# Products of 512 columns issued as two of 256, and tiles that begin at multiples of 128 bytes

## The chip, the cores and the metric

The kernel runs on one core of one Trainium2 chip. The metric is the device time of one execution in microseconds (us), taken as the median of several runs. A profiled execution lies beside them; its rows are what the prediction is worked out from.

## The reference, cut to what matters

Four transformer blocks over 512 tokens of width 1024, in float32, one after the other: block 1 has latent and windowed attention, block 2 forgetting and chunked attention, blocks 3 and 4 a mixer of convolution, sparse attention, spatial gating and pooling. After each mixer comes an output projection, then a gated feed-forward layer of width 2816, then a norm. Nearly all of the arithmetic is products of a 512 x 1024 (or 512 x 2816) activation with a weight matrix.

```
x = layer_norm(ALPHA * x + mixer(x) @ w_out)               # blocks 1, 2
x = layer_norm(ALPHA * x + (silu(x @ w_gate) * (x @ w_up)) @ w_down)
...
x = x + rms_norm(mixer(rms_norm(x)) @ w_out)               # blocks 3, 4
gu = causal_dwconv(rms_norm(x) @ w_up)
x = x + rms_norm((gelu(gu[:half]) * gu[half:]) @ w_down)
```

## The kernel before, in words

**Split operands.** A float32 matrix is carried as two tiles in the type float32r, a high part and the rest (`split`, L229). A product of two such matrices is three products on TensorE: high with high, high with low, low with high, added up in one PSUM bank of 512 float32 columns. Weights arrive by DMA in `wraw`; ScalarE casts them to `whi` (L235) and VectorE subtracts to get `wlo` (L236), for 1024 columns at a time. Activations in this form are `xh` and `xl`, 128 partitions by 8 by 512.

**Every product goes through `mm` (L270, the instruction at L271).** `mm(out, a, b)` keeps the operand `a` in the array (the kept operand; the profile shows its load as LDWEIGHTS on PEld) and moves the columns of `b` through it (the moving operand). In the rows a product is written out<-moving,kept. The kept operand is at most 128 columns wide. Those who call it:

- `fm` (L273): weights are kept, `xh` and `xl` move, all 512 tokens at once (or, from `early`, 256 of them). For each of the 8 pieces of the inner dimension it issues (wh, xh), (wh, xl), (wl, xh). The feed-forward layer of blocks 3 and 4 (`ffn`, L1298) calls it for 22 pairs of weight blocks, the mixers through `fm_tile` (L285).
- `early` (L290): the first four weight blocks of a stage are multiplied with tokens 0 to 255 first, while the last tokens are still being normalised and transposed, and then with tokens 256 to 511.
- `tok_mm` (L303): activations are kept, 128 tokens at a time, and weights move. `out_proj` (L327) uses it with both halves of 512 columns for the output projections (8 steps) and the down projections (22 steps); the kept activations are split into `pr`, `pt`, and, near the end, `piece` tiles. `tok_proj` (L312) uses it for projections by token, with columns cut at 384, 260, 320 and 332 or 512.
- `product` (L522) in `quartered` (L503): the feed-forward layer of blocks 1 and 2 as seven products per unit with 256 moving columns; three of the seven move `pr` and `pt` or `piece` tiles (operands 4, 5, 6 of `room_for`, L490), the others parts of `xh` and `xl`.

Transposes (L430, L450, L699, L886 and others) are issued beside `mm`, with 128 moving columns. The attention products are float32 or have 64 rows.

**Order.** Each engine runs its instructions in the order in which the program issues them; `behind` (L373) places the transposes of the last tokens after a given product. The weights' DMAs go through the queue of SyncE. Nothing of this order is planned by costs.

**Where tiles lie.** Three pools: constants, all SBUF tiles (`tl`, L200, and `small`, L416), and PSUM banks. A pool hands out its space by tag, in the order of first use, each tile rounded up to 32 bytes. The constants end 64 bytes past a multiple of 128. So `xh`, `xl`, `room_a` and `piece` begin 64 bytes past one; `st` (64 bytes) puts `wraw`, `whi` and `wlo` on a multiple of 128; small tiles between them put `m`, `q`, `kf`, `x`, `pr` and `pt` 32 bytes past one. Slices of 128, 256 or 512 columns are multiples of 512 bytes and change nothing in that.

Of the kernel before, what the change touches and what calls it, by code (L numbers as in the profile page):

```python
# [9 lines left out]
F32 = mybir.dt.float32  # L10
F32R = mybir.dt.float32r
# [5 lines left out]
P = 128  # L17
# [10 lines left out]


TAIL, HELD, HEAD = 4, 2, 3  # L30
LAG = 1
EARLY = (1, 2)
CONV = 4
# [155 lines left out]
class Kernel:  # L189
    def __init__(self, ctx, tc, t, out, layers=4):  # L190
        self.nc, self.tc, self.t, self.out, self.layers = tc.nc, tc, t, out, layers
        pool = lambda n, b=1, **k: ctx.enter_context(tc.tile_pool(name=n, bufs=b, **k))
        self.const = pool("const")
        self.sb = pool("sb")
        self.ps = pool("ps", space=PSUM)
        self.n = 0
        self.setup()


    def tl(self, tag, shape, dt=F32, bufs=1):  # L200
        self.n += 1
        return self.sb.tile(shape, dt, tag=tag, name=f"{tag}_{self.n}", bufs=bufs)

    def arena(self):

# [9 lines left out]
    def setup(self):  # L215
        nc, t = self.nc, self.t
        self.c = {}
        for n in ("ident", "swap", "cmp_mask", "cmp_any", "pool_cnt"):
            self.c[n] = self.const.tile(list(t[n].shape), F32, name="c_" + n)
        self.ident = self.c["ident"]  # L220
        self.mhalf = self.const.tile([P, 8], F32, name="mhalf")
        nc.vector.memset(self.mhalf, -0.5)

    def load_const(self, *names):
        for n in names:
# [42 lines left out]
        return view(hi), view(lo)  # L268

    def mm(self, out, a, b, start=True, stop=True, **k):  # L270
        self.last_mm = self.nc.tensor.matmul(out, a, b, start=start, stop=stop, **k)  # L271

    def fm(self, out, w, x, cols=None):  # L273
# [53 lines left out]
    def out_proj(self, act, nk, src, use, order, first=None):  # L327
# [36 lines left out]
        for t in range(NT):  # L364
# [3 lines left out]
            later.append(use(t, ps[t]))  # L368
            if t >= LAG and later[0]:
                self.behind(later.pop(0))  # L370
# [45 lines left out]
    def small(self, name, bufs=1):  # L416
        src = self.t[name]
        self.n += 1
        x = self.sb.tile(list(src.shape), F32, tag="s_" + name[:-1], name=f"s_{name}_{self.n}", bufs=bufs)
        self.nc.sync.dma_start(x, src)  # L420
        return x

# [1061 lines left out]
```

## Time and profile before

| | |
|---|---|
| median of 3 runs | 2369.16 us (2368.55 to 2370.86) |
| the profiled execution, its own time | 2370.62 us |
| its span, first to last instruction | 2368.9 us |
| mean granted clock of TensorE | 0.995 of full speed |
| instructions | 33153, of them 13098 products and 13098 loads |
| DMA | 227.37 MB, mean 96 GB/s |

Reading: PE is TensorE's products, PEld its loads of the kept operand, DVE is VectorE, ACT ScalarE. Ends of products are modelled, and one product's time overlaps the next one's; the distance of two starts is what the array really needs from one to the next. Where a row of the timeline stands for several instructions (x2, x8), it gives the first start and the time to the last end.

### The profile page before, as it was taken

The numbers are of one execution on the slowest core, as the hardware profiler recorded it, in microseconds if no ns is written. First come the engines' busy times: TensorE is split into PE (matmuls) and PEld (weight loads), VectorE is DVE, ScalarE is ACT, GpSimd is POOL, SyncE is SP. The second block draws the span as 40 slices with busy tenths as digits, with TensorE's granted clock in tenths as the row PEclk, the third lists the DMA queues.
The fourth block names the chain that finished last, engine by engine and source line by source line (L and its number), as shares of the span: only waits on it lengthen the run. The fifth ranks groups of instructions, "written<-read, shape, count | busy, mean of one in ns | idle before, by whom it ended". The sixth has DMA issues, their size and how long they took to land.

```text
span 2368.9 us, 33153 instructions
## 1 busy us (share of the span) xinstructions
PE 2333.6 (99%) x13098; PEld 1928.8 (81%) x13098; DVE 1483.9 (63%) x2638; ACT 1031.0 (44%) x1821; POOL 66.5 (3%) x86
## 2 busy tenths in 40 slices
PE   9999999999999999999999999999999999999998
PEld 8668999988977789998888588888878758888887
DVE  5675988735455599884478665555346866555533
ACT  4574555433455555453343544334233464334331
POOL 1001000000000010000010000000000000000000
PEclk9999999999999999999999999999999999999999
DMA  6122333431422123343323222322222322332330
GB/s 199 49 90 67 108 112 111 136 115 37 133 95 90 54 73 116 107 135 117 105 73 118 70 90 98 98 91 97 95 94 82 118 71 75 104 98 89 98 98 36
DMA packets 73979, 227.37 MB, mean 96 GB/s; under 512 B 10712, under 2 KB 13656, under 8 KB 73824
## 3 DMA queue, kind: packets, MB, share of 16 engines
q1 hardware_dynamic: 73824, 225.25, 29.6%
q8 instruction: 103, 1.69, 0.3%
q14 instruction: 52, 0.43, 0.1%
HBM read 218.81 MB, written 2.11 MB: 93 GB/s over the span
## 4 chain that ended last, share of the span: by engine, by line
PE 90%; DVE 6%; ACT 1%; issue 1%; POOL 1%; DMA 1%; SPq 0%; DVEq 0%; POOLq 0%; ACTq 0%
PE sc L271 30%; PE mm L271 27%; PE tp L271 19%; PE o L271 11%; PE tp L699 2%; DVE xl L236 1%; DVE wlo L236 1%; DVE pr L668 1%; DVE x L1354 0%; POOL lst L1352 0%; POOL ag L385 0%; DVE pr L689 0%; ACT rt L390 0%; ACT rt L1349 0%; DMA m<-cum_rows 0%
## 5 line engine op out<-in xcount | busy, mean ns | idle before, releaser
L236 DVE TENSOR_TENSOR wlo<-wraw,whi 128x1024 fp32r<-128x1024 f32 (+5 forms) x391 | 458.2, 1174 | 629.9 <-ACT whi L235 629.5
L235 ACT CAST whi<-wraw 128x1024 fp32r<-128x1024 f32 (+4 forms) x389 | 393.5, 1013 | 790.7 <-PE sc L271 433.7
L271 PE MATMUL mm<-xh,whi 128*128 128x256 f32 (+2 forms) x912 | 304.8, 335 | 4.0 <-ACT q L551 3.7
L271 PE MATMUL mm<-xh,wlo 128*128 128x256 f32 (+2 forms) x912 | 304.3, 334 | 0.0
L271 PE MATMUL mm<-xl,whi 128*128 128x256 f32 (+2 forms) x912 | 302.7, 332 | 1.1 <-DVE xl L236 1.1
L271 PEld LDWEIGHTS mm<-xh,whi 128*128 128x128 f32 (+1 forms) x912 | 172.3, 189 | 27.3 <-issue 4.8
L271 PEld LDWEIGHTS mm<-xh,wlo 128*128 128x128 f32 (+1 forms) x912 | 172.7, 189 | 20.6 <-issue 2.6
L271 PEld LDWEIGHTS mm<-xl,whi 128*128 128x128 f32 (+1 forms) x912 | 172.4, 189 | 19.6 <-DVE xl L236 1.5
L271 PE MATMUL sc<-xh,wlo 128*128 128x512 f32 (+1 forms) x416 | 146.0, 351 | 7.1 <-DVE wlo L236 7.1
L271 PE MATMUL sc<-xl,whi 128*128 128x512 f32 (+1 forms) x416 | 145.3, 349 | 0.0
L271 PE MATMUL sc<-xh,whi 128*128 128x512 f32 (+1 forms) x416 | 145.3, 349 | 0.0
L271 PE MATMUL tp<-xh,whi 128*128 128x256 f32 (+1 forms) x416 | 134.6, 324 | 0.0
L271 PE MATMUL tp<-xl,whi 128*128 128x256 f32 (+1 forms) x416 | 134.3, 323 | 0.0
L271 PE MATMUL tp<-xh,wlo 128*128 128x256 f32 (+1 forms) x416 | 134.2, 323 | 0.0
L684 ACT ACTIVATE pr<-pr,mx 128x512 f32<-128x512 f32 (+3 forms) x160 | 88.3, 555 | 69.6 <-DVE mx L682 69.6
L271 PE MATMUL sc<-pr,whi 128*128 128x256 f32 x352 | 99.0, 281 | 0.0
L271 PE MATMUL sc<-pr,wlo 128*128 128x256 f32 x352 | 98.6, 280 | 0.0
L271 PEld LDWEIGHTS sc<-xh,wlo 128*128 128x128 f32 x416 | 80.2, 193 | 18.5 <-DVE wlo L236 7.5
L271 PE MATMUL sc<-whi,pr 128*128 128x512 f32 x288 | 94.5, 395 | 0.0
L271 PEld LDWEIGHTS sc<-xh,whi 128*128 128x128 f32 x416 | 80.1, 192 | 11.0
L271 PEld LDWEIGHTS sc<-xl,whi 128*128 128x128 f32 x416 | 80.1, 192 | 11.0
L271 PE MATMUL sc<-whi,pt 128*128 128x512 f32 x264 | 86.8, 395 | 0.0
(467 smaller groups left out, 5300.3 us busy)
## 6 DMA issues: line engine op xcount, KB each, us to landing
wraw<-in_up SPq DMA_DIRECT2D x180, 512.0 KB, 3.5
wraw<-in_down SPq DMA_DIRECT2D x88, 512.0 KB, 3.4
wraw<-in_i_fm SPq DMA_DIRECT2D x20, 512.0 KB, 3.5
wraw<-in_c_fm SPq DMA_DIRECT2D x16, 512.0 KB, 3.4
wraw<-in_out SPq DMA_DIRECT2D x16, 512.0 KB, 3.5
wraw<-in_i_tok SPq DMA_DIRECT2D x16, 326.0 KB, 2.8
wraw<-in_a_out SPq DMA_DIRECT2D x8, 512.0 KB, 3.4
wraw<-in_c_out SPq DMA_DIRECT2D x8, 512.0 KB, 3.4
```

Source lines behind the costliest of these rows:

```text
L235: nc.scalar.copy(hi, src)
L236: nc.vector.tensor_sub(lo, src, hi.bitcast(F32))
L271: self.last_mm = self.nc.tensor.matmul(out, a, b, start=start, stop=stop, **k)
L668: self.nc.vector.tensor_tensor_reduce(out=h["pr"][t][:, cols], in0=sc[:, cols], in1=add, scale=1.0, scalar=-3e38, op0=ALU.add, op1=ALU.max ...
L684: nc.scalar.activation(prt[t], prt[t], AF.Exp, bias=mx[:, 1, t:t + 1], scale=scale, accum_out=mx[:, 2, t:t + 1])
L699: nc.tensor.transpose(ps[:, at:at + P], prt[t][:, P * kt:P * kt + P], self.ident)
```

## The change

A product whose kept operand is of the split type and has 128 rows, and which moves 512 columns, is issued as two instructions of 256 columns with the same kept operand. The first clears the bank where the old one did; the second adds. The last instruction is still the one that `behind` refers to. Tiles of less than 256 elements per partition, and those of `small`, move to a pool of their own behind the large ones; large tiles are padded to a multiple of 32 elements, and `mhalf` is padded so that the constants end on a multiple of 128 bytes. With that, `xh`, `xl`, `room_a`, `piece`, `wraw`, `whi`, `wlo`, `q`, `kf`, `x`, `pr` and `pt` all begin on a multiple of 128 bytes.

```diff
@@ -28,6 +28,7 @@
 
 
 TAIL, HELD, HEAD = 4, 2, 3
+PAD = 56
 LAG = 1
 EARLY = (1, 2)
 CONV = 4
@@ -192,14 +193,23 @@
         pool = lambda n, b=1, **k: ctx.enter_context(tc.tile_pool(name=n, bufs=b, **k))
         self.const = pool("const")
         self.sb = pool("sb")
+        self.tiny = pool("tiny")
         self.ps = pool("ps", space=PSUM)
         self.n = 0
         self.setup()
 
 
     def tl(self, tag, shape, dt=F32, bufs=1):
+
         self.n += 1
-        return self.sb.tile(shape, dt, tag=tag, name=f"{tag}_{self.n}", bufs=bufs)
+        n = int(np.prod(shape[1:]))
+        name = f"{tag}_{self.n}"
+        if n < 256:
+            return self.tiny.tile(shape, dt, tag=tag, name=name, bufs=bufs)
+        if n % 32 == 0:
+            return self.sb.tile(shape, dt, tag=tag, name=name, bufs=bufs)
+        x = self.sb.tile([shape[0], n + -n % 32], dt, tag=tag, name=name, bufs=bufs)[:, 0:n]
+        return x if len(shape) == 2 else x.rearrange("p (a b) -> p a b", a=shape[1])
 
     def arena(self):
 
@@ -218,8 +228,8 @@
         for n in ("ident", "swap", "cmp_mask", "cmp_any", "pool_cnt"):
             self.c[n] = self.const.tile(list(t[n].shape), F32, name="c_" + n)
         self.ident = self.c["ident"]
-        self.mhalf = self.const.tile([P, 8], F32, name="mhalf")
-        nc.vector.memset(self.mhalf, -0.5)
+        self.mhalf = self.const.tile([P, PAD], F32, name="mhalf")
+        nc.vector.memset(self.mhalf[:, 0:8], -0.5)
 
     def load_const(self, *names):
         for n in names:
@@ -268,6 +278,10 @@
         return view(hi), view(lo)
 
     def mm(self, out, a, b, start=True, stop=True, **k):
+
+        if a.dtype == F32R and a.shape[0] == P and b.shape[-1] == 512:
+            self.nc.tensor.matmul(out[:, 0:256], a, b[:, 0:256], start=start, stop=stop, skip_group_check=True)
+            out, b, start, k = out[:, 256:512], b[:, 256:512], False, dict(skip_group_check=True)
         self.last_mm = self.nc.tensor.matmul(out, a, b, start=start, stop=stop, **k)
 
     def fm(self, out, w, x, cols=None):
@@ -416,7 +430,7 @@
     def small(self, name, bufs=1):
         src = self.t[name]
         self.n += 1
-        x = self.sb.tile(list(src.shape), F32, tag="s_" + name[:-1], name=f"s_{name}_{self.n}", bufs=bufs)
+        x = self.tiny.tile(list(src.shape), F32, tag="s_" + name[:-1], name=f"s_{name}_{self.n}", bufs=bufs)
         self.nc.sync.dma_start(x, src)
         return x
```

## Rows read from the trace of the kernel before

**Rows 1.** The page's busy times, share of the span and instructions by engine

```profile
PE 2333.6 (99%) x13098; PEld 1928.8 (81%) x13098; DVE 1483.9 (63%) x2638; ACT 1031.0 (44%) x1821; POOL 66.5 (3%) x86
```

**Rows 2.** The page's chain that ended last, by engine and by line

```profile
PE 90%; DVE 6%; ACT 1%; issue 1%; POOL 1%; DMA 1%; SPq 0%; DVEq 0%; POOLq 0%; ACTq 0%
PE sc L271 30%; PE mm L271 27%; PE tp L271 19%; PE o L271 11%; PE tp L699 2%; DVE xl L236 1%; DVE wlo L236 1%; DVE pr L668 1%; DVE x L1354 0%; POOL lst L1352 0%; POOL ag L385 0%; DVE pr L689 0%; ACT rt L390 0%; ACT rt L1349 0%; DMA m<-cum_r
```

**Rows 3.** Windows: feed-forward, down projection, two mixers, quartered stage

```profile
core 0: us, PE busy (x) PEld busy (x) DVE busy (x) ACT busy (x) POOL busy (x), PEclk, DMA share, GB/s
1434.00:1656.00 222.00, 222.00 (x954) 178.84 (x953) 122.86 (x146) 84.23 (x105) 0.00 (x0) 1.00 0.30 97
1657.00:1757.00 100.00, 100.00 (x430) 80.39 (x429) 36.67 (x40) 29.98 (x38) 0.00 (x0) 1.00 0.33 105
...
627.00:845.00 218.00, 214.91 (x1081) 159.44 (x1080) 123.38 (x390) 114.76 (x263) 4.36 (x3) 1.00 0.27 87
...
1800.00:2000.00 200.00, 196.58 (x1090) 144.85 (x1090) 143.15 (x334) 88.27 (x196) 10.87 (x17) 1.00 0.28 85
...
885.00:1065.00 180.00, 180.00 (x1558) 180.00 (x1557) 161.51 (x189) 91.81 (x122) 0.00 (x0) 1.00 0.36 118
```

**Rows 4.** Waits in 1434 to 1656 (us in total, times, longest)

```profile
DVE wlo L236 <- ACT whi L235: 92.3, 39, 2.9
ACT q L1327 <- DVE q L1324: 42.3, 20, 2.1
ACT whi L235 <- PE sc L271: 27.2, 15, 3.9
```

**Rows 5.** Timeline of PE (start, us): feed-forward's first product, down projection's first

```profile
1432.69 0.39 PE L271 MATMUL tp<-xh,whi 128*128 128x512 f32 x1
...
1656.68 0.63 PE L271 MATMUL mm<-whi,pt 128*128 128x512 f32 x2
```

**Rows 6.** Timeline of PE: the product after the down projection's 432nd

```profile
1757.49 0.63 PE L271 MATMUL mm<-piece,piece 128*128 128x512 f32 x2
```

**Rows 7.** Timeline of PE in the quartered stage: first products of groups

```profile
1009.37 0.28 PE L271 MATMUL mm<-xh,whi 128*128 128x256 f32 x1
...
1012.43 0.28 PE L271 MATMUL sc<-pr,whi 128*128 128x256 f32 x1
1012.55 0.28 PE L271 MATMUL sc<-piece,whi 128*128 128x256 f32 x1
...
1015.27 0.28 PE L271 MATMUL tp<-xh,whi 128*128 128x256 f32 x1
...
1018.00 0.28 PE L271 MATMUL tp<-pr,whi 128*128 128x256 f32 x1
```

**Rows 8.** Timeline of PE: early products, and transposes of block 2

```profile
1409.62 0.28 PE L271 MATMUL mm<-xl,whi 128*128 128x256 f32 x1
...
1417.57 0.28 PE L271 MATMUL o<-xh,wlo 128*128 128x256 f32 x1
...
1418.68 0.28 PE L271 MATMUL tp<-xl,whi 128*128 128x256 f32 x1
...
587.74 1.04 PE L430 MATMUL sc<-c_ident,x 128*128 128x128 f32 x8
```

**Rows 9.** Timeline of PE: projection by token in block 2, 512 columns

```profile
640.24 0.39 PE L271 MATMUL mm<-whi,xh 128*128 128x512 f32 x1
...
644.36 0.39 PE L271 MATMUL tp<-whi,xh 128*128 128x512 f32 x1
```

**Rows 10.** Groups by shape on PEld, 1434 to 1656 (busy us, mean ns)

```profile
L271 PEld LDWEIGHTS sc<-xh,whi 128*128 128x128 f32 x120 | 22.6, 188 | 5.4
L271 PEld LDWEIGHTS sc<-xl,whi 128*128 128x128 f32 x120 | 22.6, 188 | 5.4
```

**Rows 11.** Timeline of PE: projection by token in block 2, 260 columns

```profile
602.75 0.41 PE L271 MATMUL mm<-whi,xh 128*128 128x260 f32 x2
...
603.96 0.28 PE L271 MATMUL o<-whi,xl 128*128 128x260 f32 x1
```

## The prediction

> **What bounds the kernel.** Read the busy shares first: TensorE is busy 2333.6 us of a span of 2368.9, VectorE 63%, ScalarE 44% [rows 1]. The chain of waits says the same from the other end: 90% of the span hangs on TensorE, nearly all of it on the one line that issues products [rows 2]. The windows by stage then say where there is slack: in the gated feed-forward part of block 3 and in the down projection behind it TensorE is busy 222.0 of 222.0 and 100.0 of 100.0 us; in the stages with attention it misses about 3 us in 200 [rows 3]. In the feed-forward stretch the waits are those of ScalarE and VectorE, which wait for TensorE or for each other [rows 4]. So what counts is how far apart products start. The length of a product in the rows is modelled and overlaps the next one; starts are what to subtract.
>
> **The pace of 512 columns today.** The 960 products of the feed-forward stretch begin at 1432.69, and what follows them begins at 1656.68 [rows 5]: 223.99 / 960 = 233.3 ns each. The next 432, the down projection, run to 1757.49 [rows 6]: 100.81 / 432 = 233.4 ns. In the first the activations move and the weights are kept, in the second it is the other way round.
>
> **The pace of 256 columns today.** The quartered stage has such products already. 27 starts from 1009.37 to 1012.43 [rows 7]: 113.3 ns; these move xh and xl. The next 24, which move pr and a piece tile, take until 1015.27: 118.3 ns. Then xh and xl again, 24 until 1018.00: 113.8 ns. The early products of the feed-forward stage move xh and xl as well: 70 starts from 1409.62 to 1417.57 [rows 8], 113.6 ns; but after eight transposes the same kind runs from 1418.68 to 1432.69, 119 starts, at 117.7 ns. So there are two paces, 113.3 and some 118, and 2 x 113.3 = 226.6 lies below 233.3 while 2 x 117.7 = 235.4 lies above it.
>
> **Does it matter where a tile begins?** Compare two kinds of product that move whi and wlo, which begin on a multiple of 128 bytes. Where the kept operand is xh or xl (64 bytes past one), 18 starts from 640.24 to 644.36 give 228.9 ns [rows 9]. Where it is pr or pt (32 bytes past), it is the 233.4 of the down projection. With 256 columns the slow group moves pr, 32 bytes past, and the fast one xh. Both point the same way: 32 bytes past costs 4 to 5 ns. The Trainium skill (TensorE: Matmul & The Clock Gate, Step-by-step: what each phase is for) says that loading the next weights takes no read bandwidth from the running product, since they have ports of their own; by that alone the start of the kept tile would change nothing. The rows here disagree by 4.5 ns a product, and the measurement decides. No row shows both operands on a multiple of 128 bytes, which is what the change makes of nearly all.
>
> **The change, part by part.**
> *Splitting.* By the code 5736 products have a split kept operand of 128 rows and 512 columns: 1920 in the feed-forward of blocks 3 and 4 (2 x 20 x 2 x 24), 2112 in four down projections (22 x 24 each), 768 in four output projections (8 x 24), 936 in the mixers. Each becomes two, with a weight load each: today a product that keeps the same whi as the one before still has its own load record, 120 for 120 [rows 10], so none is saved. I take 113.3 ns for a half, the pace of the longer fast stretch, since both operands will begin at least as evenly as there. That gives 233.3 - 226.6 = 6.7 ns a product. In the 4800 outside the mixers all of it counts, TensorE waiting for nothing there: 32.2 us. In the mixers some of it turns into waits for softmax and evictions; I take half of 936 x 6.7: 3.1 us.
> *Aligning.* The products that move pr, pt or a piece in the quartered stage (3 of 7 per unit, 11 units, 2 layers, 24 each: 1584) go from 118.3 to 113.4: 7.8 us. VectorE is busy 161.5 of 180.0 us there [rows 3]; taking 4 us off a stage of about 220 leaves it room. The slow part of five early blocks, 5 x 119 x 4.3 = 2.6 us, may keep its pace, being on the same tiles as the fast part; half: 1.3 us.
> *The rest costs nothing.* Padding and the second pool move no instruction; the eight columns of mhalf in use are set as before. The second half of a product accumulates into columns that its own bank's start already cleared, as the quartered stage does. More instructions to fetch and issue: the quartered stage issues a load and a product every 113 ns and TensorE is busy without a gap [rows 3], so the cover is there; if it failed, the pace of a half would show it, and the slow rival below prices that. What is late next is nobody in the long stages: weights land and are split well ahead, with ScalarE waiting on TensorE for free buffers [rows 4].
> *Sum.* 32.2 + 3.1 + 7.8 + 1.3 = 44.4 us. The profiled execution took 2370.62, 1.5 above the median of 2369.16. 2370.6 - 44.4 = 2326.2, against the median 2324.8: I say 2325.
>
> **Bounds of the unknown.** The pace of a half with both operands aligned is bounded below by the closest-packed full products in the trace, transposes of 128 columns with a weight load each: eight in 1.04 us, the last lasting 0.28 [rows 8], (1.04 - 0.28) / 7 = 109 ns. Two halves would take 218, 15.3 less than today: 15.3 x (4800 + 468) = 80.6 us, and the 256-column products that exist (4656 by the code) would gain 9.3 ns in 1584 and about 5 in the others, another 30 us: 2259. The bound above is the nearest pair that shares a kept operand and moves neighbouring columns, the two times 260 of a projection: ten starts from 602.75 to 603.96 [rows 11], 121 ns, 119.1 at 256 columns: 4.9 more than today per product, x 5268 = 25.8 us, with nothing from alignment: 2395. I take 113.3 as the nearest in columns and in tiles.
>
> **Rivals.**
> *Better than the fast pace.* If the 4 ns between the fast pace and the 109 ns of the transposes are also owed to tiles that begin 64 bytes past, the halves fall towards 109: between 2259 and 2317. For: 32 bytes past is slower than 64, so 0 may be faster still. Against: the fast pace is very regular over whole stages, like a limit of its own. Chance 0.18.
> *Part of the way.* Stretches that follow transposes keep 117.7, others run at 113.3; then about half the sum or less is left: 2335 to 2364. For: the early block [rows 8], where one disturbance changed the pace for 119 products of the same tiles. Chance 0.15.
> *The slow pace wins.* The feed-forward and down stretches follow directly on the slow early block; if its pace holds on through them, each product costs 235.4, so 2.1 x 5268 = 11 us more: 2380; at the pace of the 260-column pair, 2395. It decides at 116.65 ns a half: above that the split loses. That is a fixed cost for each product, paid twice. For: the same tiles, 64 bytes past, showed it for 14 us on end. Against: the slow group of 24 at 1012.43 was followed at once by the fast pace, and the fast stretches are the more numerous. The Trainium skill (the same page, Back-to-back issue gap) has the starts of warm products 2.5 ns plus their columns apart, 215.8 ns for 512 and 109.2 for 256, so a split would lose 2.5 ns and the kernel 14 us (an estimate from that page); its 215.8 is not what the trace shows (233.3), though its order is this rival's. Chance 0.16.
> *No change.* The split loses what alignment gains, or the tiles do not come to lie where the padding means them to, with halves near 116.5: within 4.7 us. By the sizes the constants end at byte 4096 and each large tile is a multiple of 128, so I see no reason for it. Chance 0.09.
>
> **From these to the numbers.** The forecast itself, 2317 to 2335, has 0.42. Faster: 0.42 + 0.18 + 0.15 = 0.75. A measurement of this kernel can tell about 0.2%, 4.7 us, from no change; within that 0.09; slower 0.16. The range 2285 to 2375 leaves out the lower part of the better case (0.07) and most of the slow one (0.13). The forecast's own range is 2317 to 2335.
>
> **What would show it.** The feed-forward stretch of block 3 should hold 1920 products of 256 columns, 113.3 ns apart, in 217.5 us instead of 224.0; the down projection 864 in 97.9 instead of 100.8; in the quartered stage pr, pt and piece should move at the pace of xh. TensorE's count should rise by 5736, to 18,834, with as many weight loads, their busy share rising from 81% [rows 1] to nearly that of the products, and the granted clock should stay at 1.00, the level of 2.4 GHz, where it is so now [rows 3]. Halves above 116.65 ns, or gaps between load and product that today do not exist, would make the prediction wrong; so would products that keep 118 ns with both operands aligned.

## The result and the profile after

The changed kernel takes 2432.55 us (median of 4 runs, 2432.2 to 2434.85) beside 2368.86 for the kernel before: a ratio of 1.0269 (95% interval 1.0253 to 1.0285), 63.7 us slower. The forecast of 2325 had the wrong sign, and the range ended 58 us too low.

The page of the changed kernel, busy times and the chain by engine; its span is 2431.1 us, its mean granted clock 0.994:

```profile
PE 2393.3 (98%) x18834; PEld 2265.4 (93%) x18834; DVE 1485.6 (61%) x2638; ACT 1029.7 (42%) x1821; POOL 68.9 (3%) x86
...
PE 92%; DVE 5%; ACT 1%; issue 1%; DMA 1%; POOL 1%; DVEq 0%; POOLq 0%; SPq 0%; ACTq 0%
```

The counts are those announced, 18,834 products and as many loads. The other engines do what they did [rows 1]; the chain hangs on TensorE for 92% instead of 90% [rows 2]. So no new wait has appeared. TensorE is simply busy for longer.

The windows of the changed kernel, feed-forward of block 3 and its down projection (columns as in [rows 3]):

```profile
1471.00:1699.00 228.00, 228.00 (x1902) 228.00 (x1901) 122.26 (x145) 83.63 (x105) 0.00 (x0) 1.00 0.32 95
1700.00:1803.00 103.00, 103.00 (x859) 102.85 (x858) 36.64 (x40) 29.87 (x38) 0.00 (x0) 1.00 0.34 103
```

As before TensorE is busy from end to end, at a granted clock of 1.00, the level of 2.4 GHz. The loads are busy without a gap too, 228.00 of 228.00 us, but so they were in the quartered stage of the kernel before, 180.00 of 180.00, at 113 to 118 ns a product [rows 3]. The slowdown is neither a stall nor the clock. Of the loads in that stretch, grouped by shape:

```profile
L283 PEld LDWEIGHTS sc<-xh,whi 128*128 128x128 f32 x120 | 23.0, 192 | 0.0
L285 PEld LDWEIGHTS sc<-xh,whi 128*128 128x128 f32 x120 | 23.0, 192 | 0.0
```

L283 is the first half and L285 the second. Both have their own load of the same kept operand, as the prediction read from [rows 10]; the split saves none. What has changed is the distance of two starts. The timeline of PE in the changed kernel: first products of three groups of 24 in the quartered stage, then the feed-forward's first product, the down projection's first, and the product after its last:

```profile
920.12 0.28 PE L285 MATMUL tp<-pr,whi 128*128 128x256 f32 x1
...
923.01 0.28 PE L285 MATMUL mm<-xh,whi 128*128 128x256 f32 x1
...
925.88 0.29 PE L285 MATMUL sc<-pr,whi 128*128 128x256 f32 x1
...
1469.23 0.28 PE L283 MATMUL tp<-xh,whi 128*128 128x256 f32 x1
...
1699.63 0.28 PE L283 MATMUL mm<-whi,pt 128*128 128x256 f32 x1
...
1803.50 0.28 PE L283 MATMUL mm<-piece,piece 128*128 128x256 f32 x1
```

The feed-forward takes 230.40 us for 1920 halves, 120.0 ns each; two make 240.0, where the whole product took 233.3 [rows 5]. The down projection takes 103.87 for 864, 120.2 ns. In the quartered stage, where nothing is split, groups of 24 take 2.89 and 2.87 us, 120 ns a product, whether they move `pr` or `xh`; in the kernel before it was 113.3 for `xh` and 118.3 for `pr` [rows 7]. So two things went wrong: the halves are slow, and the products that already had 256 columns became slow too, though only their tiles have moved.

Where the 62.2 us of the span come from, by the sum of the start distances of each kind of product in the two traces: the 5736 products that were split went from 1362.7 to 1407.1 us, 44.4 more (240.0 - 233.3 = 6.7 ns each would be 38.4; most of the rest is in the mixers); the 3072 quartered and early products that move `xh` or `xl` from 376.0 to 390.6, 14.6 more; the 1584 that move `pr`, `pt` or `piece` from 187.3 to 190.8, 3.5 more. Together that is 62.5. All other products took 434.4 us in both.

### The profile page after: what moved, and what is told of

It reads as the page before. It is cut to its first block, busy times and chain, and to the rows that moved or that the text cites. A ratio compares the mean times of both kernels' runs of the same rounds, so it can differ in the third digit from the quotient of the medians.

```text
span 2431.1 us, 44665 instructions
## 1 busy us (share of the span) xinstructions
PE 2393.3 (98%) x18834; PEld 2265.4 (93%) x18834; DVE 1485.6 (61%) x2638; ACT 1029.7 (42%) x1821; POOL 68.9 (3%) x86
## 4 chain that ended last, share of the span: by engine, by line
PE 92%; DVE 5%; ACT 1%; issue 1%; DMA 1%; POOL 1%; DVEq 0%; POOLq 0%; SPq 0%; ACTq 0%
PE sc L285 22%; PE mm L285 18%; PE tp L285 14%; PE mm L283 10%; PE sc L283 9%; PE o L285 8%; PE tp L283 6%; PE o L283 3%; PE tp L713 2%; DVE pr L682 1%; DVE wlo L246 0%; DVE xl L246 0%; DVE pr L703 0%; PE sc L444 0%; ACT rt L404 0%
## 5 line engine op out<-in xcount | busy, mean ns | idle before, releaser
L285 PE MATMUL mm<-xh,whi 128*128 128x256 f32 (+1 forms) x912 | 259.7, 285 | 2.0 <-ACT q L565 2.0
L285 PE MATMUL mm<-xh,wlo 128*128 128x256 f32 (+1 forms) x912 | 259.4, 284 | 0.0
L285 PE MATMUL mm<-xl,whi 128*128 128x256 f32 (+1 forms) x912 | 259.2, 284 | 0.0
L285 PEld LDWEIGHTS mm<-xh,whi 128*128 128x128 f32 (+1 forms) x912 | 174.6, 191 | 3.1 <-ACT q L565 2.9
L285 PEld LDWEIGHTS mm<-xh,wlo 128*128 128x128 f32 (+1 forms) x912 | 174.4, 191 | 2.6 <-issue 2.5
L285 PEld LDWEIGHTS mm<-xl,whi 128*128 128x128 f32 (+1 forms) x912 | 174.4, 191 | 1.3 <-issue 1.1
L285 PE MATMUL sc<-xh,wlo 128*128 128x256 f32 x416 | 120.0, 289 | 8.2 <-DVE wlo L246 8.2
L285 PE MATMUL tp<-xh,wlo 128*128 128x256 f32 x416 | 118.0, 284 | 3.3 <-DVE wlo L246 3.3
L285 PE MATMUL sc<-xl,whi 128*128 128x256 f32 x416 | 119.7, 288 | 1.4 <-DVE xl L246 1.4
L285 PE MATMUL sc<-xh,whi 128*128 128x256 f32 x416 | 119.5, 287 | 0.0
L285 PE MATMUL tp<-xh,whi 128*128 128x256 f32 x416 | 118.4, 285 | 0.0
L285 PE MATMUL tp<-xl,whi 128*128 128x256 f32 x416 | 117.9, 283 | 0.0
L283 PE MATMUL mm<-xh,whi 128*128 128x256 f32 (+1 forms) x400 | 116.3, 291 | 0.0
L283 PE MATMUL mm<-xh,wlo 128*128 128x256 f32 (+1 forms) x400 | 114.9, 287 | 0.0
L283 PE MATMUL mm<-xl,whi 128*128 128x256 f32 (+1 forms) x400 | 114.3, 286 | 0.0
L285 PE MATMUL sc<-pr,whi 128*128 128x256 f32 x352 | 99.8, 284 | 0.0
L285 PE MATMUL sc<-pr,wlo 128*128 128x256 f32 x352 | 99.7, 283 | 0.0
L285 PEld LDWEIGHTS sc<-xh,wlo 128*128 128x128 f32 x416 | 81.6, 196 | 8.6 <-DVE wlo L246 8.6
L285 PEld LDWEIGHTS sc<-xl,whi 128*128 128x128 f32 x416 | 81.4, 196 | 1.8 <-DVE xl L246 1.8
```

Source lines behind the costliest of these rows:

```text
L283: self.nc.tensor.matmul(out[:, 0:256], a, b[:, 0:256], start=start, stop=stop, skip_group_check=True)
```

## Experiments

All of them do the whole computation. A distance, below, is the number of bytes by which the start of the kept operand that is loaded during a product (the next product's) lies past the start of the operand that this product moves, taken within 256 bytes, by the addresses that the allocator gave the tiles. Slices of 128, 256 or 512 columns do not change it. In the changed kernel the distance is 0 for all products of split operands, and its large tiles begin on multiples of 256 bytes, not only of 128.

**1. The split alone.** The kernel before, with the change's edit to `mm` and tiles where they were:

```diff
     def mm(self, out, a, b, start=True, stop=True, **k):
+        if a.dtype == F32R and a.shape[0] == P and b.shape[-1] == 512:
+            self.nc.tensor.matmul(out[:, 0:256], a, b[:, 0:256], start=start, stop=stop, skip_group_check=True)
+            out, b, start, k = out[:, 256:512], b[:, 256:512], False, dict(skip_group_check=True)
```

> The split alone, every tile where it was before. Theory P (placement: the pace is set by how the starts of the moving and the kept operand lie to each other within 128 bytes; equal starts are the slow case, 120 ns a half): the products that move xh and xl stay 64 bytes apart, halves at 113.3 to 117.7 ns; those of the output and down projections are 32 apart, halves near 118; the sum is -14 to +12 us, 2355 to 2381. Theory S (the split itself costs: two products in a row with the same kept operand take 120 ns each wherever they lie): 6.7 ns more per split product, about +35 us, 2404.

Measured: 2399.85 us, ratio 1.0127 (1.0097 to 1.0156). Timeline of PE: feed-forward's first product, down projection's first, and the product after it:

```profile
1449.41 0.28 PE L273 MATMUL tp<-xh,whi 128*128 128x256 f32 x1
...
1675.55 0.28 PE L273 MATMUL mm<-whi,pt 128*128 128x256 f32 x1
...
1779.43 0.28 PE L273 MATMUL mm<-piece,piece 128*128 128x256 f32 x1
```

Halves of 226.14 / 1920 = 117.8 ns in the feed-forward and 103.88 / 864 = 120.2 in the down projection, both above 116.65, below which a split would pay. About half of the loss is here without any alignment. The time misses theory P's 2355 to 2381 by 19 us and comes close to theory S's 2404; the next run shows why S does not hold all the same.

**2. The alignment alone.** The changed kernel with the three lines in `mm` taken out.

> The alignment alone, products of 512 columns left whole. Theory P: the 256-column products of the quartered stage and of the early blocks fall from 113.3 or 118 to 120 ns, +21 us; the whole products, now with equal starts, take up to 240 ns, up to +35 us; 2390 to 2425. Theory S: nothing is split, so whole products stay at 233.3 and the time at 2362 to 2372.

Measured: 2358.74 us, ratio 0.9953 (0.9931 to 0.9976). Timeline of PE: three groups of the quartered stage, then feed-forward and down projection as above:

```profile
921.95 0.28 PE L281 MATMUL tp<-xh,whi 128*128 128x256 f32 x1
...
924.83 0.28 PE L281 MATMUL tp<-pr,whi 128*128 128x256 f32 x1
...
927.71 0.28 PE L281 MATMUL mm<-xh,whi 128*128 128x256 f32 x1
...
1439.36 0.40 PE L281 MATMUL tp<-xh,whi 128*128 128x512 f32 x1
...
1656.99 0.39 PE L281 MATMUL mm<-whi,pt 128*128 128x512 f32 x1
...
1755.05 0.61 PE L281 MATMUL mm<-piece,piece 128*128 128x512 f32 x2
```

This run decides most. The same 960 products of 512 columns now take 217.63 us, 226.7 ns each instead of 233.3, and the 432 of the down projection 98.06, 227.0. But both quartered groups take 2.88 us, 120.0 ns, with no split anywhere. So the slow 256-column products are no effect of splitting, for which theory S has no place; theory P had them right, but let the whole products slow down to 240 ns, and its 2390 to 2425 was missed as well. Equal starts help 512 columns and hurt 256: by the sums of start distances the whole products gained 29.6 us and those of 256 columns lost 17.5. Split and alignment do not add up either: alone they cost +30.2 and -10.9 us, together +63.7.

**3. `pr` and `pt` 64 bytes past, products whole.** One unused tile of 32 bytes ahead of `pr` in the kernel before:

```diff
     def tl(self, tag, shape, dt=F32, bufs=1):
+        if tag == "pr" and not self.gap:
+            self.gap = self.sb.tile([P, 8], F32, tag="gap", name="gap", bufs=1)
```

> No split; a gap of 32 bytes ahead of pr moves pr and pt from 32 to 64 bytes past a multiple of 128, so that all activations lie 64 bytes from the weights. Theory P: the output and down projections take the 228.9 ns of the projection by token instead of 233.3 (2880 products, -13 us), pr and pt in the quartered stage move at the pace of xh (1584 products, -7.8 us): 2348. Theory S: no change, 2369.

Measured: 2359.15 us, ratio 0.9958 (0.9936 to 0.998). Timeline of PE, the down projection's first product and the one after it:

```profile
1651.75 0.40 PE L274 MATMUL mm<-whi,pt 128*128 128x512 f32 x1
...
1750.72 0.40 PE L274 MATMUL mm<-piece,piece 128*128 128x512 f32 x1
```

98.97 / 432 = 229.1 ns instead of 233.4 [rows 6]. Here only the place of `pr`, `pt` and what lies behind them moved: a distance of 160 became 192. In the quartered stage the products that move `pr` or `pt` went from a distance of 96 to 64 and from 117.7 to a mean of 115.5 ns. The feed-forward, whose distance of 64 is untouched, keeps 233.3. The time, in eight runs from 2354.33 to 2370.77, lies between the two theories' 2348 and 2369.

**4. The same, with the split.**

> The same gap, with the split. Theory P: all split products are 64 bytes apart; with halves at 113.3 ns the time is 2325, with halves at 117.7 ns about 2373. Theory S: halves at 120 ns, about 2390 (35 us more than whole, less what the gap gains).

Measured: 2377.23 us, ratio 1.0045 (1.0024 to 1.0066). Timeline of PE, first and following product of the down projection in block 1 and in block 3:

```profile
449.52 0.28 PE L276 MATMUL mm<-whi,pt 128*128 128x256 f32 x1
...
546.54 0.28 PE L276 MATMUL mm<-piece,piece 128*128 128x256 f32 x1
...
1655.23 0.28 PE L276 MATMUL mm<-whi,pt 128*128 128x256 f32 x1
...
1757.28 0.28 PE L276 MATMUL mm<-piece,piece 128*128 128x256 f32 x1
```

Block 1: 97.02 / 856 = 113.3 ns. Block 3: 102.05 / 864 = 118.1, on the same tiles at the same distance of 192. The feed-forward keeps 117.8 throughout. So at 64 and 192 a half has two paces, and here one of them holds for a whole stretch.

**5. All large tiles 64 bytes past.** The changed kernel with `PAD = 40` instead of 56: all of them move together, and the distances are as in the changed kernel.

> The changed kernel with 16 elements less behind mhalf, so that every large tile begins 64 bytes past a multiple of 128: all starts equal as before, none on a multiple. Theory R (only the distance between the starts of the moving and the kept operand counts): halves stay at 120 ns, 2432. Theory A (the multiple itself counts, for the kept or the moving operand): halves leave 120 ns, and with 113 to 118 the time is 2365 to 2415.

Measured: 2435.63 us in one run. Timeline of PE, the down projection's first product and the one after it:

```profile
1703.39 0.28 PE L283 MATMUL mm<-whi,pt 128*128 128x256 f32 x1
...
1807.27 0.28 PE L283 MATMUL mm<-piece,piece 128*128 128x256 f32 x1
```

103.88 / 864 = 120.2 ns, as in the changed kernel. For halves a multiple of 128 bytes means nothing by itself; how the two operands lie to each other does. For whole products no run did the same.

**6. Whole products at equal starts, products of 256 columns at 64.** The second run's kernel, with the weights of the quartered stage and of `early` begun 64 bytes into tiles that are 128 bytes longer:

```diff
-            hi = self.tl("whi", [P, 1024], F32R, 4)
-            lo = self.tl("wlo", [P, 1024], F32R, 4)
+            hi = self.tl("whi", [P, 1056], F32R, 4)[:, 16:1040]
+            lo = self.tl("wlo", [P, 1056], F32R, 4)[:, 16:1040]
```

> Alignment without the split, and the weights of the products that have 256 columns anyway (quartered stage, early blocks) begin 64 bytes past a multiple of 128, everything else on one. Theory R: whole products keep the 226.9 ns of the alignment alone, those with 256 columns go from 120 to between 113.3 and 117.7 ns: 4656 x 2.3 to 6.6 = 11 to 31 us less than the 2358.7 of the alignment alone, 2328 to 2348. Theory A: a kept operand off the multiple is no better, 2359 or more.

Measured: 2347.74 us, ratio 0.9905 (0.9884 to 0.9927). The quartered and early products ran at a mean of 113.3 to 114.7 ns, but of the whole ones, for which theory R had 226.9 ns, a part had slowed. Timeline of PE in the feed-forward, first products of groups:

```profile
1495.17 0.39 PE L281 MATMUL o<-xh,whi 128*128 128x512 f32 x1
...
1500.75 0.39 PE L281 MATMUL tp<-xh,whi 128*128 128x512 f32 x1
...
1511.64 0.40 PE L281 MATMUL sc<-xh,whi 128*128 128x512 f32 x1
```

5.58 us for 24 products, 232.5 ns, then 10.89 for 48, 226.9. Tiles of 4224 bytes lie 128 further within 256 from one to the next, and the two paces go by it: at a distance of 0 a mean of 227.4 (1278 products that move `xh` or `xl`), at 128 one of 232.4 (1272). So 128 is no equal start; the distance counts within 256 bytes.

**7. The split with the weights 64 bytes in.** The changed kernel with all of `whi` and `wlo` as in the diff above, so that distances are 64 and 192 in turn.

> The changed kernel, split, with all weights that go through whi and wlo 64 bytes past a multiple of 128 and all activations on one. Theory R: as in the split with the activations 64 bytes past (2377), halves at 113 to 118 ns instead of 120: 2365 to 2390. Theory A: halves at 120 where the moving or the kept operand is off a multiple, 2420 or more.

Measured: 2367.02 us in one run. Timeline of PE, feed-forward's first product, down projection's first, and the product after it:

```profile
1436.65 0.28 PE L283 MATMUL tp<-xh,whi 128*128 128x256 f32 x1
...
1654.25 0.28 PE L283 MATMUL mm<-whi,pt 128*128 128x256 f32 x1
...
1756.30 0.28 PE L283 MATMUL mm<-piece,piece 128*128 128x256 f32 x1
```

217.60 / 1920 = 113.3 ns: the pace and the 217.5 us that the prediction announced, with the starts apart and not together. The down projection has 118.1. Moving the weights by 64 bytes, with as many products and loads, takes the changed kernel back by 65 us.

**8. As 6, with tiles of 1088 elements,** 4352 bytes, a multiple of 256, so that every whole product has a distance of 0 and every quartered one 64.

> Whole products; weight tiles 4352 bytes apart instead of 4224, so that the distance from the moving operand to the kept one that is loaded meanwhile is 0 within 256 bytes for every product of 512 columns and 64 for those of 256. Theory D (the distance within 256 bytes sets the pace; whole products want 0, where they take 226.9 ns, those of 256 columns want 64): all whole products return from 230 to 227 ns, those with 256 columns stay at 114: 2328 to 2338. Theory R (within 128 bytes): as with the weights 4224 bytes apart, 2344 to 2350.

Measured: 2332.86 us, ratio 0.9865 (0.9833 to 0.9897), faster than both kernels. The page's busy times, and the timeline of PE as for the second run:

```profile
PE 2291.7 (98%) x13098; PEld 1918.5 (82%) x13098; DVE 1482.9 (64%) x2638; ACT 1030.2 (44%) x1821; POOL 66.7 (3%) x86
```

```profile
921.91 0.28 PE L281 MATMUL sc<-pr,whi 128*128 128x256 f32 x1
...
924.63 0.28 PE L281 MATMUL tp<-xh,whi 128*128 128x256 f32 x1
...
927.35 0.28 PE L281 MATMUL tp<-pr,whi 128*128 128x256 f32 x1
...
1413.01 0.39 PE L281 MATMUL tp<-xh,whi 128*128 128x512 f32 x1
...
1630.63 0.62 PE L281 MATMUL mm<-whi,pt 128*128 128x512 f32 x2
...
1728.69 0.39 PE L281 MATMUL mm<-piece,piece 128*128 128x512 f32 x1
```

Groups of 24 in 2.72 us, 113.3 ns; the feed-forward 217.62 / 960 = 226.7 ns; the down projection 98.06 / 432 = 227.0. Each kind has its own best distance, and no product is split. Tiles 4352 bytes long lie 256 further within 512 from one to the next, and the pace no longer alternates: 256 apart is as good as 0. Three of the four runs lie within 2.5 us, the fourth took 2347.42.

**9. As 8, with the quartered and early weights 128 bytes in.**

> The same with a distance of 128 instead of 64 for the products of 256 columns. Theory D: 128 differs from 0, the products of 256 columns leave 120 ns; which way is open: 109 to 118 gives 2310 to 2352. Theory R: 128 is 0, so 120 ns and 2355 to 2362.

Measured: 2356.03 us, ratio 0.9942 (0.9922 to 0.9962). Timeline of PE, first products of two groups in the quartered stage:

```profile
1052.41 0.28 PE L281 MATMUL mm<-xh,whi 128*128 128x256 f32 x1
...
1055.26 0.28 PE L281 MATMUL sc<-xh,whi 128*128 128x256 f32 x1
```

2.85 / 24 = 118.8 ns; the mean over the quartered and early products that move `xh` or `xl` is 119.1. For 256 columns 128 is nearly as bad as 0. The time lies in theory R's 2355 to 2362, 4 us past theory D's 2352; that 128 differs from 0 rests on the whole products of run 6, 232.4 against 227.4.

**10. The split, all weights 128 bytes in** (tiles of 1088 elements, slices from element 32).

> The changed kernel, split, with weight tiles 128 bytes past a multiple of 256 and activations on one. Theory D: halves leave 120 ns; at 113.3 the time is about 2340, at 118 about 2400. Theory R: 2432, halves at 120.

Measured: 2414.6 us, ratio 1.0189 (1.0169 to 1.021). Timeline of PE, the down projection's first product and the one after it:

```profile
1687.01 0.28 PE L283 MATMUL mm<-whi,pt 128*128 128x256 f32 x1
...
1789.78 0.28 PE L283 MATMUL mm<-piece,piece 128*128 128x256 f32 x1
```

102.77 / 864 = 118.9 ns; the products that move `xh` or `xl` have a mean of 118.7. As in the ninth run 128 lies between 0 and 64, and the time lies between theory D's 2400 and theory R's 2432.

**11. The split, all weights 64 past a multiple of 256** (tiles of 1088, slices from element 16).

> The changed kernel, split, with weight tiles 64 bytes past a multiple of 256 and activations on one. Theory D: products that move activations have a distance of 64, those that move weights 192; the first at 114 ns, the second at 116 to 118: 2355 to 2380. Theory R: the same, 2367 as with the weights 4224 bytes apart.

Measured: 2388.3 us, ratio 1.0078 (1.0057 to 1.01). Timeline of PE, feed-forward's first product and the down projection's first:

```profile
1445.40 0.28 PE L283 MATMUL tp<-xh,whi 128*128 128x256 f32 x1
...
1671.54 0.28 PE L283 MATMUL mm<-whi,pt 128*128 128x256 f32 x1
```

226.14 / 1920 = 117.8 ns, where the seventh run had 113.3; the time is 8 us past the 2380 that was expected at most. The distance of 64 allows the fast pace and does not bring it about: here a steady 64 did worse than 64 and 192 in turn. The quartered stages show the two paces at one and the same distance of 64; timeline of PE, first products of two neighbouring groups of 24 in block 1, then in block 2:

```profile
301.18 0.28 PE L285 MATMUL tp<-pr,whi 128*128 128x256 f32 x1
...
303.90 0.28 PE L285 MATMUL mm<-xh,whi 128*128 128x256 f32 x1
...
940.61 0.28 PE L285 MATMUL tp<-xh,whi 128*128 128x256 f32 x1
...
943.44 0.28 PE L285 MATMUL tp<-pr,whi 128*128 128x256 f32 x1
```

2.72 / 24 = 113.3 and 2.83 / 24 = 117.9 ns, and each stage keeps its pace to the end. The start distances of the other runs add when a pace changes on the way. In runs 4, 8 and 11, where the distance stays the same for a whole stretch, no stretch of 60 or more products changed from one pace to the other. In runs 6 and 7, where it goes from 64 to 192 or back from one weight tile to the next, it happened 27 times, each within a dozen or so products of such a step, though most steps changed nothing.

**12. The fourth kernel, with the product that clears a bank left whole,** in the feed-forward the first of every group of 24.

> As the split kernel with pr and pt 64 bytes past a multiple of 128, but the first product of every group of 24 (the one that clears the bank) stays one instruction of 512 columns; the other 23 are two halves each. The question is what picks 113.3 or 117.8 ns for a half whose operands lie 64 bytes apart. Theory E (the pace is set when a run of products of 256 columns begins, and a product of 512 begins a new run each time): the halves of the feed-forward part leave the 117.8 that they kept from the early block on, some groups at 113.3; all at 113.3 would make a group of 24 take 233.3 + 46 x 113.3 = 5.45 us and the 40 groups 217.8. Rival F (a whole product changes nothing, the pace comes from where the tiles lie): 233.3 + 46 x 117.8 = 5.65 us for a group, 226.1 for the 40. The time is then about 2365 by E and 2377 by F.

Measured: 2391.86 us in one run. Timeline of PE, first products of two groups in the feed-forward:

```profile
1501.47 0.40 PE L280 MATMUL sc<-xh,whi 128*128 128x512 f32 x1
...
1507.12 0.40 PE L280 MATMUL sc<-xh,whi 128*128 128x512 f32 x1
```

5.65 us a group, the rival's figure: a whole product in between leaves the halves at 117.8. The time missed the rival's by 15 us: the down projections of blocks 1 and 2 and the quartered stage of block 2, at 113.3 in the fourth run, ran at 117.8 here at the same distances of 192 and 64, some 3400 products at 4.5 ns.

What the runs give together, ns from one start to the next:

| distance, bytes | 512 columns | 256 columns |
|---|---|---|
| 0 | 226.7 (runs 2 and 8) | 120.0 (changed kernel, runs 2 and 5) |
| 64 | 233.3 (before, run 3) | 113.3 or 117.8, by the stretch (before, runs 1, 4, 7, 8, 11, 12) |
| 96 | none | 117.7 (before) |
| 128 | 232.4 (run 6, moving `xh` or `xl`) | 118.7 to 119.3 (runs 9, 10) |
| 160 | 233.3 (before) | 120.0 (run 1) |
| 192 | 228.9 to 230.4 (before, run 3) | 113.3 or 117.8, by the stretch (runs 4, 6, 7, 11, 12) |

By the first row the split of a whole product at equal starts costs 2 x 120.0 - 226.7 = 13.3 ns; times 5736 that is 76.3 us, and the changed kernel stands 73.8 above the second run.

The first row has an exception. Near the end of an output or down projection the products of two `piece` tiles come three to six in a row at a distance of 0, among others at other distances. 113 of them took a mean of 232.0 ns in the kernel before, where both tiles begin 64 bytes past a multiple of 256, and 231.0 in run 6, where both begin on one; in run 2, with a distance of 0 all around, they took 227.2. So a few products at 0 do not reach the pace by themselves. Nor is it shown that whole products at equal starts off a multiple of 256 would reach it: every long stretch at 226.7 had both operands on one.

## Why the prediction was wrong

**What held.** TensorE bounds the kernel, start distances are the thing to subtract, the counts of products and loads, no load saved, the clock at 1.00, no new wait. The padding and the second pool cost nothing: what is neither split nor a product of 256 columns took 434.4 us before and after. The point from which a split loses, 116.65 ns a half, also held: with halves at 117.8 and 120 the first run lost, and with 113.3 in the feed-forward and 118 in the down projections the seventh came out near the time before.

**The step that failed** is "I take 113.3 ns for a half, the pace of the longer fast stretch, since both operands will begin at least as evenly as there". A half took 120.0, and the gain of 32.2 us with its 3.1 in the mixers became a loss of 44.4 us.

**Why it failed** lies one part earlier, in "32 bytes past costs 4 to 5 ns". [rows 9] and [rows 7] were read as the price of one tile's start past a multiple of 128 bytes. They are as well the price of a distance between two tiles: 192 in [rows 9] against 160 in the down projection, 64 against 96 in the quartered stage. The trace before could not tell these two readings apart, since in all four `whi` and `wlo` lay on a multiple of 128. Run 5 tells them apart for halves: everything 64 past, same distances, same 120 ns. Run 6 does it for whole products: both operands on a multiple of 128, but 128 apart, and 232.4 ns. In the prediction's own terms, the fast stretches lay at a distance of 64, where 113.3 can be had, and the change took them to a distance of 0, where every half takes 120.0.

**Alignment.** "from 118.3 to 113.4: 7.8 us" became 120.0, 3.5 us lost, and the 3072 other products of 256 columns, which the sum left where they were but for 1.3 us, lost 14.6. Where alignment does help, in whole products (233.3 to 226.7, run 2), the sum had no term, because the split takes those products away. Neither edit was priced in the state that the other one leaves.

**The bounds.** The upper one, 119.1 ns from the pair of 260 columns, was short by 0.9 ns; about half of the 37 us that its 2395 missed is that it took "nothing from alignment" where 18.1 us were lost. 109 ns was reached nowhere; 113.3 is the least that a product of 256 columns showed.

**The rivals.** The slow one, at 0.16, had the sign and the deciding point, and its place: in the first run the feed-forward did keep the pace of the early block, 117.8. Its reading as a fixed cost for each product does not hold: the feed-forward stretch took 217.60 us as 1920 halves in the seventh run and 217.62 as 960 whole products in the eighth. What the prediction said would show it wrong, "products that keep 118 ns with both operands aligned", is what the quartered stage now shows, at 120.

**Loads beside products.** The Trainium skill (TensorE: Matmul & The Clock Gate, Step-by-step: what each phase is for) gives the loads a read port of their own, so that a load takes nothing from the running product. The prediction set the measurement above it, rightly as to the fact: between the kernel before and run 2 no product differs but in where tiles lie, and the 512-column pace moves by 6.6 ns. The Trainium skill (the same page, Back-to-back issue gap) gives 215.8 and 109.2 ns for products of 512 and 256 columns, as the gap of a product by itself, and about 131 ns for 512 columns in a stream of loads and products. No run reached any of these, the least being 226.7 and 113.3.

**What stays open.** Why the distance acts, a conflict of two reads for instance, no view of the trace shows. Nor is it settled what picks 113.3 or 117.8 at distances of 64 and 192 when a stretch begins: the tiles alone do not (run 4, blocks 1 and 3; run 11, blocks 1 and 2), and a whole product in between does not (run 12). The transposes ahead of a stretch, as [rows 8] suggested, do not decide it alone either: in run 8 four stretches of 118 early products at a distance of 64 follow eight transposes each, and three ran at 117.8, one, from 1763.79, at 113.4.

## What to carry to other kernels

When TensorE is busy without a gap, look at where the moving operand and the kept operand loaded beside it begin relative to each other, within 256 bytes: moving tiles alone was worth 6.6 ns in 233 here, and 37 us of the whole kernel in run 8; and the best distance measured for 512 columns is, with 160, the worst for 256. Before the pace of one kind of product is carried over to another, check that everything that sets it, the places of both operands included, will be the same there. Two edits that act on one resource are priced together: each in the state that the other leaves.

## What the runs showed that was not expected

- Products of the same shape on the same data ran from 113.3 to 120.0 ns (256 columns) and from 226.7 to 233.3 (512), with nothing changed but where tiles lie.
- At a steady distance of 64 or 192 a stretch of 856 to 1920 halves held 113.3 or 117.8 throughout, and where the pace changed, the distance had just changed. The kernels with products at these distances spread more from run to run: 2375.63 to 2390.21 us in the fourth, where the kernel before stayed within 2368.34 and 2373.2.
- Tiles 4224 bytes long, an innocent padding by 128 bytes, made the pace alternate between 226.9 and 232.5 ns from one weight tile to the next.
